# Turning attention probabilities with VectorE squares and a round trip through DRAM in place of TensorE transposes, in a two-layer decoder trunk

## The chip, the core and the metric

The kernel runs on one NeuronCore of a Trainium2 chip. The metric is the device time of one execution in microseconds (us). Engines are called by their names in the profile: PE is TensorE's matmuls, PEld its weight loads, DVE is VectorE, ACT is ScalarE, POOL is GpSimd, and SP is the engine that issues nearly all DMAs.

## What is computed

A decoder trunk of two layers over 256 positions of width 1024. Each layer adds to the residual, in this order, a mixer (self-attention with 16 heads of width 64), a cross-attention with 4 heads into a memory of 256 rows, and a gated MLP with a short convolution. The change concerns the mixer of the second layer, called layer 1 in the code, which is the forgetting attention of the reference:

```python
qpos = start + jnp.arange(Q_BLOCK)
s = (jnp.einsum('bhtd,bhsd->bhts', qb, k).astype(jnp.float32) * scale
     + cb[..., None] - c[:, :, None, :])
s = jnp.where(key_pos[None, :] <= qpos[:, None], s, NEG_INF)
p = jax.nn.softmax(s, axis=-1).astype(v.dtype)
return jnp.einsum('bhts,bhsd->bhtd', p, v)
```

`c` is a running sum of log forget gates. The softmax runs over keys. The last product sums over keys too, so on TensorE the probabilities are needed with keys on the partitions, while the softmax wants queries on the partitions. Between the two, each head's probabilities have to be turned. With the causal mask, a head has 128 queries that see 128 keys and 128 queries that see 256 keys: a tile of 128 partitions x 384 columns, which is three blocks of 128x128.

## The kernel before

Weights come from DRAM as blocks of 128x1024 float32 (512 KB), each loaded by one DMA of SP into a tile `raw` (7 buffers). `block` (line 127) loads one and splits it into a rounded part `whi` on ACT (line 135) and a remainder `wlo` on DVE (line 136), with 5 buffers each. A projection (`proj`, `proj_nat`) of 24 matmuls of 256 columns (line 347) uses them. `HALVES` (line 38) lists for some projections one matmul that is issued as two of 128 columns (line 345).

PE's instructions stand in the order of the program (`manual_schedule` near the end of `trunk`); the other engines' instructions are ordered by a scheduler, with the program's order as priority, and each engine then runs its own list strictly in order. SP's list holds the weight loads and all other DMAs.

`mixer` (line 650) works through the 16 heads as 8 pairs. A `Pipe` counts steps; a step ends with each projection (`pipe.tick()`), 2.72 us apart. In layer 1 the steps end, in this order, with: v0 (two steps), q1, k1, q2, k2 (step 6), v1 twice, q3 (9), k3 (10), q4 (11), k4, q5 (13), k5 (14), v2 twice (15, 16), q6, k6, q7 (19), k7 (20), v3 twice (21, 22), two projections of memory keys (23, 24), and the first output projections (25 and on). Here q3 is the query projection of pair 3, which holds two heads, and v1 the values of pairs 2 and 3.

`VISITS` (line 32) says at which step PE leaves the projections for attention work, and `visit` (line 671) does it. An entry is (step, out, prod, weigh), each a tuple of pairs:

- prod: `Soft.products` (line 459) multiplies queries by keys in plain float32, two matmuls for each head, into a PSUM bank `sc`. `Soft.scores` follows on other engines: DVE adds the decay and the mask and finds the maximum (line 468), ACT takes the exponential and its sum (line 472), DVE scales by the reciprocal of the sum (line 475). The result is the tile `s2` (`self.p`).
- weigh: `Soft.weigh` (line 477) has PE turn the tile by three 128x128 transposes into PSUM for each head (line 479), and ACT or DVE copy the result to a tile `pt` (line 481).
- out: `heads_out` (line 489) multiplies `pt` by the values (line 494), and ACT and DVE split the result into `gh` and `gl` (lines 499 and 501) for the output projection.

In layer 1, each couple of pairs goes through prod at steps 6, 11, 16 and 21, through weigh at 9, 14, 19 and 24, and through out at 11, 16, 21 and 26. `evac_row` (lines 396 and 398) brings q and k from PSUM on DVE; there are three PSUM banks `acc` for projections. `s2` and `pt` have four buffers of 384 columns each. The decay rows `bc` are read from DRAM by SP (line 614), and POOL works them up (line 615).

In the cross-attention (`cross`, line 868), `scores` makes the products of four heads with `Cross.products` (line 840), two matmuls of 256 columns for each head. They stand four matmuls into a projection of values, whose other 20 follow.

Late in layer 1's MLP, `move_blocks` (line 953) moves 32x32 squares between two on-chip tiles with 32 DMAs of 256 pieces of 128 bytes each (line 959); `turn_blocks` (line 950) turns 32x32 squares on DVE just before. `swap` (line 564) of layer 0 moves 32 partitions of 1024 bytes in each DMA (line 567).

Of the kernel before, what the change touches and what calls it, by code (L numbers as in the profile page):

```python
# [17 lines left out]
P = 128  # L18
# [62 lines left out]
def trunk(ctx: ExitStack, tc: tile.TileContext, a: dict, out: bass.AP):  # L81
# [45 lines left out]
    def block(src, cols=BLK, pieces=2):  # L127
        raw = wraw.tile([P, BLK], F32, tag="raw", name="raw")
        hi = wsp.tile([P, BLK], F32R, tag="whi", name="whi")
        lo = wsp.tile([P, BLK], F32R, tag="wlo", name="wlo")  # L130
        nc.sync.dma_start(raw[:, :cols], src)
# [12 lines left out]
        return Block(hi, lo)  # L144
# [270 lines left out]
    class Stick:  # L415
# [24 lines left out]
        def weigh(self, copy):  # L440
            z = self.z
            for sp in self.sp:
                nc.tensor.matmul(z, tri, sp, **ADD)  # L443
            for sp in self.sp:
                nc.tensor.matmul(z[:, P:T], negones, sp[:, T:384], **ADD)
            self.pt = tmp.tile([P, 384], F32, tag="pt", name="pt", bufs=4)
            nc.scalar.activation(self.pt, z, AF.Exp)

    class Soft:
# [11 lines left out]
        def scores(self):  # L461
# [3 lines left out]
            p = self.p = tmp.tile([P, 384], F32, tag="s2", name="s2", bufs=4)  # L465
# [11 lines left out]
        def weigh(self, copy):  # L477
            for c in (0, P, T):
                nc.tensor.transpose(self.s[:, c:c + P], self.p[:, c:c + P], ident)  # L479
            self.pt = tmp.tile([P, 384], F32, tag="pt", name="pt", bufs=4)  # L480
            copy(self.pt, self.s)


    def both_products(heads):
        steps = [hd.products() for hd in heads]
        while steps:
            steps = [i for i in steps if next(i, i) is not i]
# [162 lines left out]
    def mixer(layer, st, xs):  # L650
# [10 lines left out]
        heads = [None] * 8  # L661
# [9 lines left out]
        def visit(out, prod, weigh):  # L671
# [4 lines left out]
            for n in prod:  # L676
                q, k, _ = pairs[n]
                heads[n] = [Stick(i, q, k) if layer == 0 and n < 4 else
                            Soft(i, q, k, decays[2 * n + i] if decays else None) for i in range(2)]
            both_products([hd for n in prod for hd in heads[n]])  # L680
# [7 lines left out]
            for n in prod:  # L688
                for hd in heads[n]:
                    hd.scores()  # L690

# [9 lines left out]
        for g in range(4):  # L701
            def pair(i, hooks=({}, {})):
                wi = w[6 * g + 4 * i:6 * g + 4 * i + 2]
                pr = 2 * g + i
                q = early if layer == 0 and g == 1 and i == 0 else proj(block(wi[0]), 0, xs, accA(), hooks=hooks[0],
                                                                        halve=halves(f"q{pr}"))
                if hooks[0]:
                    return q, lambda: proj(block(wi[1]), 0, xs, accA(), hooks=hooks[1], halve=halves(f"k{pr}"))
# [8 lines left out]
                k = proj(b[3] if layer == 0 and g == 1 and i == 0 else block(wi[1]), 0, xs, accA(),  # L717
# [61 lines left out]
            def values():  # L779
                b = [block(w[6 * g + 2]), block(w[6 * g + 3])]  # L780
# [15 lines left out]
        ks = mem_keys(layer, ms, pipe)  # L796
# [3 lines left out]
        while j < 4:  # L800
            b = block(w_out[j])
# [12 lines left out]
        bo = [block(w_out[j])]  # L814
        for i in range(j, KD):
            if i < KD - 1:
                bo.append(block(w_out[i + 1]))
# [7 lines left out]
    def mem_keys(layer, ms, pipe):  # L825
        ks = []
        for i in range(2):
            ps = proj(block(a["xa_k"][layer, i]), 0, ms, accA(), halve=() if i else HALVES[layer].get("mk", ()))
# [4 lines left out]
    class Cross:  # L833
# [3 lines left out]
        def products(self):  # L837
            s = self.s = bank(psS, "sc")
            for t in range(2):
                nc.tensor.matmul(s[:, t * T:(t + 1) * T], self.q[:, t * P:(t + 1) * P], self.k, start=t == 0,  # L840
                                 stop=True, skip_group_check=True)
# [26 lines left out]
    def cross(layer, st, xs, ms, ks):  # L868
# [167 lines left out]
    def down_rows(gs, acc, spare):  # L1036
# [22 lines left out]
        def square(ps, s, scale=1.0):  # L1059
            n = ps.shape[1]  # L1060
            x = wide("sq") if n > 384 else tmp.tile([P, 384], F32, tag="s2", name="sq", bufs=4)
# [154 lines left out]
```

## Time and profile before

| | us |
|---|---|
| median of 3 runs | 648.34 (648.24 to 648.74) |
| profiled execution | 648.27 |
| span of that execution, first to last instruction | 646.5 |
| busy in the span: PE / DVE / ACT / POOL | 640.0 / 533.1 / 433.3 / 71.4 |

The page gives times in microseconds. Matmuls are pipelined: the length of one matmul in the trace is longer than the distance to the next, so a stream is read from its starts, or from the chain of waits, which merges equal instructions into pieces with a start, a length and a count. A DMA has two times: how long SP is busy with issuing it, and how long after that the data has landed. All times below are on the clock of the profiled execution, from its first instruction.

### The profile page before, as it was taken

What the parts mean: (1) busy time and instruction counts of PE and PEld (TensorE: products, weight loads), DVE (VectorE), ACT (ScalarE), POOL (GpSimd) and SP (SyncE); (2) the same over time, 40 slices, a digit from 0 to 9 for tenths busy, and PEclk for the clock granted to TensorE, in tenths of its full rate; (3) what the DMA queues carried; (4) which work ended last, traced back from release to release, by engine and by line L of the source; (5) the groups of instructions that cost most, each with busy time, mean ns of one, the idle gap of its engine ahead of it and who ended that gap; (6) DMA issues with size and microseconds to landing.
All of it is one profiled execution on the core that took longest, in us unless ns stands there. A gap on an engine that the chain in (4) does not pass through costs nothing.

```text
span 646.5 us, 14603 instructions
## 1 busy us (share of the span) xinstructions
PE 640.0 (99%) x5629; PEld 626.5 (97%) x5629; DVE 533.1 (82%) x1116; ACT 433.3 (67%) x871; POOL 71.4 (11%) x83
## 2 busy tenths in 40 slices
PE   9999999999999999999999999999999999999996
PEld 7999999999999999999999999999999999999996
DVE  7769995999999999766588987779999999996442
ACT  7689864688787676644464776557878666774332
POOL 0001000317000000011003220022450000000000
PEclk9999999999999999999999999999999999999999
DMA  8975751545556676666638754325365577595501
GB/s 338 388 273 196 268 190 46 195 153 204 185 169 219 210 216 181 182 194 199 212 126 301 254 179 139 131 86 180 122 236 193 165 225 201 163 357 197 193 2 66
DMA packets 47669, 125.07 MB, mean 193 GB/s; under 512 B 13520, under 2 KB 17392, under 8 KB 47600
## 3 DMA queue, kind: packets, MB, share of 16 engines
q1 hardware_dynamic: 47456, 123.88, 58.4%
q8 instruction: 44, 0.72, 0.4%
q10 hardware_dynamic: 144, 0.26, 0.1%
q14 instruction: 25, 0.20, 0.1%
HBM read 120.95 MB, written 1.07 MB: 189 GB/s over the span
## 4 chain that ended last, share of the span: by engine, by line
PE 98%; issue 1%; ACT 0%; DVE 0%; POOLq 0%; POOL 0%; DVEq 0%
PE acc L347 50%; PE sc L347 29%; PE acc L1053 3%; PE sc L1053 3%; PE po L1053 2%; PE po L494 2%; PE po L347 2%; PE sc L459 1%; PE sc L479 1%; PE sc L840 1%; PE sc L863 1%; PE acc L250 1%; PE sc L443 1%; PE po L899 0%; PE acc L345 0%
## 5 line engine op out<-in xcount | busy, mean ns | idle before, releaser
L136 DVE TENSOR_TENSOR wlo<-raw,whi 128x512 fp32r<-128x512 f32 (+2 forms) x288 | 267.6, 951 | 55.3 <-ACT whi L135 53.6
L135 ACT ACTIVATE whi<-raw 128x512 fp32r<-128x512 f32 (+2 forms) x288 | 225.4, 815 | 85.0 <-PE acc L347 34.1
L347 PE MATMUL sc<-xn,whi 128*128 128x256 f32 x656 | 112.9, 276 | 0.0
L347 PEld LDWEIGHTS sc<-xn,whi 128*128 128x128 f32 x656 | 98.6, 188 | 0.0
L347 PE MATMUL sc<-xn,wlo 128*128 128x256 f32 x328 | 90.5, 276 | 0.0
L347 PE MATMUL acc<-xh,whi 128*128 128x256 f32 x288 | 81.0, 281 | 0.0
L347 PE MATMUL acc<-xn,whi 128*128 128x256 f32 x464 | 80.3, 276 | 0.0
L347 PE MATMUL acc<-xl,whi 128*128 128x256 f32 x288 | 79.7, 277 | 0.0
L347 PE MATMUL acc<-xh,wlo 128*128 128x256 f32 x282 | 78.1, 277 | 0.0
L347 PEld LDWEIGHTS acc<-xn,whi 128*128 128x128 f32 x464 | 69.8, 188 | 0.0
L347 PE MATMUL acc<-gh,whi 128*128 128x256 f32 x240 | 66.9, 279 | 0.0
L347 PE MATMUL acc<-gl,whi 128*128 128x256 f32 x240 | 66.1, 277 | 0.0
L347 PE MATMUL acc<-gh,wlo 128*128 128x256 f32 x236 | 65.1, 276 | 0.0
L347 PE MATMUL acc<-xn,wlo 128*128 128x256 f32 x232 | 64.0, 276 | 0.0
L267 POOL TENSOR_TENSOR sq<-sq 128x256 f32<-128x256 f32 x35 | 30.1, 859 | 302.0 <-ACT sq L261 280.7
L347 PEld LDWEIGHTS sc<-xn,wlo 128*128 128x128 f32 x328 | 61.6, 188 | 0.0
L347 PEld LDWEIGHTS acc<-xh,whi 128*128 128x128 f32 x288 | 54.1, 188 | 0.4
L347 PEld LDWEIGHTS acc<-xl,whi 128*128 128x128 f32 x288 | 54.2, 188 | 0.0
L347 PEld LDWEIGHTS acc<-xh,wlo 128*128 128x128 f32 x282 | 53.0, 188 | 0.4 <-issue 0.4
L347 PEld LDWEIGHTS acc<-gh,whi 128*128 128x128 f32 x240 | 45.1, 188 | 1.1 <-ACT gh L185 0.8
L347 PEld LDWEIGHTS acc<-gl,whi 128*128 128x128 f32 x240 | 44.9, 188 | 0.0
L347 PEld LDWEIGHTS acc<-gh,wlo 128*128 128x128 f32 x236 | 44.3, 188 | 0.0
(310 smaller groups left out, 1536.7 us busy)
## 6 DMA issues: line engine op xcount, KB each, us to landing
raw<-up SPq DMA_DIRECT2D x88, 512.0 KB, 3.9
raw<-fox_in SPq DMA_DIRECT2D x24, 512.0 KB, 4.2
raw<-down_rows SPq DMA_DIRECT2D x22, 512.0 KB, 4.5
raw<-ab_in SPq DMA_DIRECT2D x20, 512.0 KB, 6.6
raw<-down SPq DMA_DIRECT2D x16, 448.0 KB, 3.5
raw<-ab_out SPq DMA_DIRECT2D x8, 512.0 KB, 4.8
raw<-down SPq DMA_DIRECT2D x8, 512.0 KB, 3.5
raw<-fox_out SPq DMA_DIRECT2D x8, 512.0 KB, 4.4
```

Of the source, the lines that this page charges most:

```text
L135: i = nc.scalar.activation(hi[:, s], raw[:, s], AF.Copy)
L136: j = nc.vector.tensor_sub(lo[:, s], raw[:, s], hi[:, s].bitcast(F32))
L250: nc.tensor.matmul(ps, w.broadcast_to([P, P]), w.broadcast_to([P, 512]), start=True, stop=True)
L267: nc.gpsimd.tensor_tensor(sq, sq, self.acc, op=ALU.add)
L347: nc.tensor.matmul(ps, st, mv, **kw)
L443: nc.tensor.matmul(z, tri, sp, **ADD)
L459: nc.tensor.matmul(s[:, c], q[:, qs], k[:, 0:n], start=i == 0, stop=True, skip_group_check=True)
L479: nc.tensor.transpose(self.s[:, c:c + P], self.p[:, c:c + P], ident)
L494: nc.tensor.matmul(po[i * DH:(i + 1) * DH, j * T + q:(j + 1) * T], v[m][:, vc + i * DH:vc + (i + 1) * DH], hd.pt[:, c], start=m == 0 and j ...
L840: nc.tensor.matmul(s[:, t * T:(t + 1) * T], self.q[:, t * P:(t + 1) * P], self.k, start=t == 0, stop=True, skip_group_check=True)
L863: nc.tensor.transpose(self.s[:, m * T + t * P:m * T + (t + 1) * P], self.p[:, t * T + m * P:t * T + (m + 1) * P], ident)
L1053: nc.tensor.matmul(ps[:, o:o + T], x[:, s], y[:, c + o:c + o + T], start=False, stop=k == KF - 1 and x is gl, skip_group_check=True)
```

## The change

Layer 1's probabilities of pairs 0 to 5 are no longer turned by PE. DVE turns each 32x32 square of a pair's tile in place (`nc.vector.transpose`), once for each pair, at the end of its scores. Four DMAs of SP for each pair then store the tile to DRAM (`store`, the entry's new field `away`), and four DMAs fetch it back (`fetch`, field `back`) into `pt`, so that the squares land in their turned places. A store DMA takes 32 partitions and writes 768 pieces of 128 bytes; a fetch DMA reads 192 pieces of 512 bytes. The last couple of pairs, 6 and 7, is still turned by PE at step 24.

The visits of layer 1 become: prod at 6, 11, 16 and 21 as before; out one round later, at 16, 21, 24 and 26; stores at 10, 15 and 20; fetches at 13, 19 and 22. Standalone visits of PE at 9, 14 and 19 are gone. Tiles `s2` and `pt` become two buffers of 768 columns, one for a pair.

In layer 1's mixer, weight loads are written six blocks ahead in the program (`weights`, `loads`), and each store and fetch is ordered behind the last load written so far. The pace of the loads is still set by the buffers of `raw`.

Matmuls issued in halves: in layer 1, the entry of `v2` goes and one for `k4` comes. In the cross-attention of both layers, the second row block of the last two heads' products is issued as two matmuls of 128 columns.

```diff
-          ((6, (), (0, 1), ()), (9, (), (), (0, 1)), (11, (0, 1), (2, 3), ()), (14, (), (), (2, 3)),
-           (16, (2, 3), (4, 5), ()), (19, (), (), (4, 5)), (21, (4, 5), (6, 7), ()), (24, (), (), (6, 7)),
-           (26, (6, 7), (), ())))
+          ((6, (), (0, 1), ()), (10, (), (), (), (0, 1)), (11, (), (2, 3), ()), (13, (), (), (), (), (0, 1)), (15, (), (), (), (2, 3)),
+           (16, (0, 1), (4, 5), ()), (19, (), (), (), (), (2, 3)), (20, (), (), (), (4, 5)),
+           (21, (2, 3), (6, 7), ()), (22, (), (), (), (), (4, 5)), (24, (4, 5), (), (6, 7)), (26, (6, 7), (), ())))
+TURNED = ((), (0, 1, 2, 3, 4, 5))
...
-          {"k0": (5,), "q1": (2,), "v1": (2,), "v2": (3,), "q6": (2,), "mk": (2,), "o2": (2,)})
+          {"k0": (5,), "q1": (2,), "v1": (2,), "k4": (2,), "q6": (2,), "mk": (2,), "o2": (2,)})
...
+    def of_pair(tag):
+        both = tmp.tile([P, 768], F32, tag=tag, name=tag, bufs=2)
+        return both, [both[:, i * 384:(i + 1) * 384] for i in range(2)]
+
+    def store(both, behind):
+        away = far.tile([32, 4 * 768], F32, tag="turn", name="turn", bufs=6)
+        to = away.rearrange("c (n i r) -> c n i r", i=4, r=32)
+        for i in range(4):
+            x = both[i * 32:i * 32 + 32].rearrange("c (n r) -> c n r", r=32)
+            order(nc.sync.dma_start(to[:, :, i], x), behind)
+        return away
+
+    def fetch(away, behind):
+        both, halves = of_pair("pt")
+        away = away.rearrange("c (s f q) -> c s f q", f=4, q=P)
+        for f in range(4):
+            i = nc.sync.dma_start(both[f * 32:f * 32 + 32].rearrange("c (s q) -> c s q", q=P), away[:, :, f])
+            order(i, behind)
+        return halves
...
+        def weights(src):
+            if layer == 0:
+                return block(src)
+            begun.append(src)
+            while len(loads) < min(len(begun) + 6, len(uses)):
+                loads.append(load(uses[len(loads)]))
+            return block(None, raw=loads[len(begun) - 1][0])
...
+            for n in away:
+                tiles[n] = store(tiles[n], loads[-1][1])
+            for n in back + weigh:
+                for hd, pt in zip(heads[n], fetch(tiles[n], loads[-1][1]) if n in back else of_pair("pt")[1]):
+                    hd.pt = pt
...
+                if n in TURNED[layer]:
+                    nc.vector.transpose(tiles[n], tiles[n])
...
-            both_products(hd[2:])
+            both_products(hd[2:], ((0, 0, T), (1, 0, P), (1, P, T)))
```

More of the change, by code (lines that the diff above doesn't have):

```diff
@@ L125, in fence, with load, block @@
         fences.append([skip, on_act, on_dve])
-    def block(src, cols=BLK, pieces=2):
+    def load(src, cols=BLK):
         raw = wraw.tile([P, BLK], F32, tag="raw", name="raw")
+        return raw, nc.sync.dma_start(raw[:, :cols], src)
+    def block(src, cols=BLK, pieces=2, raw=None):
+        if raw is None:
+            raw, _ = load(src, cols)
         hi = wsp.tile([P, BLK], F32R, tag="whi", name="whi")
         lo = wsp.tile([P, BLK], F32R, tag="wlo", name="wlo")
-        nc.sync.dma_start(raw[:, :cols], src)
         step = cols // pieces
@@ L660, in mixer @@
         pairs, turned = [None] * 8, [None] * 8
-        heads = [None] * 8
+        heads, tiles = [None] * 8, [None] * 8
+        first_soft = 0 if layer else 4
         def launch(pr, q, k, v):
@@ L669, in launch, with visit @@
                     pipe.at(d + (pr in (4, 6)), lambda x=x, r=r: (rope_sum if pr > 4 else rope)(x, r))
-        def visit(out, prod, weigh):
+        uses = [6 * g + i for g in range(4) for i in ((0, 1, 2, 3, 4, 5), (0, 1, 4, 5, 2, 3))[g > 1]]
+        uses = [w[i] for i in uses] + [a["xa_k"][layer, i] for i in range(2)] + [w_out[i] for i in range(KD)]
+        loads, begun = [], []
+        def weights(src):
[5 more added lines that the diff above has]
+            return block(None, raw=loads[len(begun) - 1][0])
+        def visit(out, prod, weigh, away=(), back=()):
             if out:
@@ L704, in pair @@
                 pr = 2 * g + i
-                q = early if layer == 0 and g == 1 and i == 0 else proj(block(wi[0]), 0, xs, accA(), hooks=hooks[0],
+                q = early if layer == 0 and g == 1 and i == 0 else proj(weights(wi[0]), 0, xs, accA(), hooks=hooks[0],
                                                                         halve=halves(f"q{pr}"))
                 if hooks[0]:
-                    return q, lambda: proj(block(wi[1]), 0, xs, accA(), hooks=hooks[1], halve=halves(f"k{pr}"))
+                    return q, lambda: proj(weights(wi[1]), 0, xs, accA(), hooks=hooks[1], halve=halves(f"k{pr}"))
                 if layer == 0 and pr > 4:
@@ L716, in pair @@
                 pipe.tick()
-                k = proj(b[3] if layer == 0 and g == 1 and i == 0 else block(wi[1]), 0, xs, accA(),
+                k = proj(b[3] if layer == 0 and g == 1 and i == 0 else weights(wi[1]), 0, xs, accA(),
                          halve=halves(f"k{pr}"))
@@ L779, in values @@
             def values():
-                b = [block(w[6 * g + 2]), block(w[6 * g + 3])]
+                b = [weights(w[6 * g + 2]), weights(w[6 * g + 3])]
                 for t in range(2):
@@ L795, in mixer @@
         assert len(ms) == KD
-        ks = mem_keys(layer, ms, pipe)
+        ks = mem_keys(layer, ms, pipe, weights)
         nst, nxt = Stats(one=True), Normed(h, G_XA + 8 * layer, "x", NX, 2)
@@ L800, in mixer @@
         while j < 4:
-            b = block(w_out[j])
+            b = weights(w_out[j])
             n = min(7, sum(o is not None for o in outs))
@@ L823, in mixer, with mem_keys @@
         return nst, nxt.res, ms, ks
-    def mem_keys(layer, ms, pipe):
+    def mem_keys(layer, ms, pipe, weights):
         ks = []
         for i in range(2):
-            ps = proj(block(a["xa_k"][layer, i]), 0, ms, accA(), halve=() if i else HALVES[layer].get("mk", ()))
+            ps = proj(weights(a["xa_k"][layer, i]), 0, ms, accA(), halve=() if i else HALVES[layer].get("mk", ()))
             ks.append(evac_row(ps, mem, "mk", False))
@@ L835, in __init__, with products @@
             self.q, self.k, self.st = q[HALF[i]], k[HALF[i]], st
-        def products(self):
+        def products(self, cuts=((0, 0, T), (1, 0, T))):
             s = self.s = bank(psS, "sc")
-            for t in range(2):
-                nc.tensor.matmul(s[:, t * T:(t + 1) * T], self.q[:, t * P:(t + 1) * P], self.k, start=t == 0,
-                                 stop=True, skip_group_check=True)
+            for t, c, e in cuts:
+                nc.tensor.matmul(s[:, t * T + c:t * T + e], self.q[:, t * P:(t + 1) * P], self.k[:, c:e],
+                                 start=t == c == 0, stop=True, skip_group_check=True)
                 yield
```

18 lines of the change are left out of this document (10 added, 8 removed).

## The prediction, written before the change was run

> **What bounds the kernel now.** I read the page first, then the chain of waits in order of time around the second mixer and the cross-attentions, then DVE, SP and the landing times of DMAs there. The page:
>
> ```profile
> span 646.5 us, 14603 instructions
> PE 640.0 (99%) x5629; PEld 626.5 (97%) x5629; DVE 533.1 (82%) x1116; ACT 433.3 (67%) x871; POOL 71.4 (11%) x83
> PE 98%; issue 1%; ACT 0%; DVE 0%; POOLq 0%; POOL 0%; DVEq 0%
> ```
>
> PE is never waiting for long: 98% of the chain that ended last is PE's own work. Time is saved only by giving PE less work or letting the same matmuls follow each other more tightly, and it is saved fully only while nobody else becomes late. The chain in the second mixer and in both cross-attentions (start, length, what, count):
>
> ```profile
> 128.39 2.56 PE po L347 x20
> 130.95 2.83 PE acc L347 x24
> ...
> 347.44 1.51 PE sc L459 x16
> 348.95 0.43 PE acc L347 x2
> 349.38 0.17 PE acc L345 x2
> 349.55 7.99 PE acc L347 x69
> 357.54 1.31 PE sc L479 x12
> 358.85 5.46 PE acc L347 x48
> 364.30 1.45 PE po L494 x16
> 365.76 1.51 PE sc L459 x16
> 367.26 8.38 PE acc L347 x72
> 375.64 1.31 PE sc L479 x12
> 376.95 0.36 PE acc L347 x3
> 377.31 0.17 PE acc L345 x2
> 377.48 5.04 PE acc L347 x44
> ...
> 393.98 1.31 PE sc L479 x12
> 395.29 5.47 PE acc L347 x48
> ...
> 437.12 5.44 PE sc L347 x48
> ...
> 445.28 2.56 PE po L347 x20
> 447.83 2.83 PE acc L347 x24
> ```
>
> Two readings. A visit that turns two pairs is 12 transposes in 1.31 us, 109 ns each. And the weight stream has two rhythms: 48 matmuls in 5.44 us are 113 ns each, while 24 in 2.83 us are 118 ns each. The slower one sets in after some switch between float32 and rounded work and stays until something shifts the stream; issuing one matmul in halves does that and costs next to nothing.
>
> **The change, part by part.**
>
> *Transposes removed.* Three visits (357.54, 375.64, 393.98) of 1.31 us: 3.93 us off PE's path. Nothing on PE replaces them.
>
> *Switches removed.* Each visit also disturbed the stream behind it. 48 matmuls cost 5.44 us when clean. After the first visit they took 5.46 (0.02 more); after the second 0.36 + 0.17 + 5.04 = 5.57 (0.13 more); after the third 5.47 (0.03 more). Together 0.18 us.
>
> *Out moved.* The product with the values (1.45 us) leaves step 11 and comes in at step 24, ahead of the transposes of the last couple. Its matmuls are the same; one float32 block is split off and another is joined on. I charge 0.1 us for a different switch, between 0 and 0.2.
>
> *Rhythm of the longer stretches.* Before, 69 matmuls at 349.55 took 7.99 us where 69 x 0.1133 = 7.82 are clean: a slow run of 0.17 us. Now five projections in a row follow each visit. If such a run begins in one of them it lasts until the next visit: at 0.11 us for 24 matmuls (2.83 less 2.72), up to 0.55 for each of three stretches. The entries at v1, k4 and q6 are issued in halves, which should start them clean. I charge 0.2, with bounds of -0.17 (the old run goes) and 1.65.
>
> *Cross scores in halves.* After the scores of a cross-attention, 20 + 24 matmuls run in the slow rhythm: 44 x 4.5 ns = 0.2 us in each layer. The second mixer's products end in 128-column matmuls and one stretch after them, the 72 at 367.26, is nearly clean (8.38 against 8.16, of which 0.11 is the entry). With the same ending I expect most of it back: 0.3 us for both layers, bounds 0 and 0.4. The four added instructions split streaming that is there anyway: about 0.
>
> *DVE's six turns.* A row for 256 columns exists:
>
> ```profile
> L951 DVE STREAM_TRANSPOSE mem<-h x8: 437/443/445, 493.3 to 528.2; 128x256 f32<-128x256 f32 x8
> 347.20:419.00 71.80, 71.80 (x651) 68.50 (x649) 59.63 (x195) 48.06 (x136) 13.74 (x16) 1.00 0.57 191
> ```
>
> 768 columns are three of these, 1.3 us at most; if part of the 0.44 is a fixed cost they are cheaper. Six are at most 8 us. The second row is the windows view for the second mixer: 71.80 us, of which DVE (its third figure) is busy 59.63. With 8 us more in a stage that is 4 us shorter, DVE would have 67.6 of 67.7 us: full, but not over. It hides because weight splits run several blocks ahead of PE, so lateness is absorbed; at zero cover each missing microsecond is PE's. ACT loses the copies of the three visits, which hides nothing on PE.
>
> *Stores and fetches on SP.* These DMAs' forms do not occur before. The nearest rows:
>
> ```profile
> 543.41 14.79 SPq L959 DMA_DIRECT2D h<-mem  x22
> ...
> L959 SPq DMA_DIRECT2D h<-mem x32: 591/608/1281, 528.8 to 557.6; - x32
> ...
> DMA to landing us min/median/max: 1.9/2.2/4.6
> ...
> L567 SPq DMA_DIRECT2D turned<-q x16: 507/582/1186, 50.1 to 80.7; - x16
> ...
> L131 SPq DMA_DIRECT2D raw<-fox_in x24: 328/328/516, 298.8 to 364.5; - x24
> ```
>
> A DMA of 256 pieces of 128 bytes (line 959) keeps SP for 0.61 us and the next follows after 0.67; one of 32 pieces (line 567) keeps it for 0.58; a weight load for 0.33. So eight times the pieces cost 0.03 us, and I take 0.7 us for a store of 768 pieces. Bounds: 0.33 (the load) and 2.0 (three pitches of 0.67, if pieces do set it). For a fetch of 192 pieces I take 0.65. Landing on chip took 2.2 us in the middle; through DRAM there are two rows, the store of the gate sums and the reads of the decays:
>
> ```profile
> L605 SPq DMA_DIRECT2D decay<-fc x1: 343/343/343, 339.3 to 339.3; - x1
> ...
> DMA to landing us min/median/max: 4.0/4.0/4.0
> ...
> L614 SPq DMA_DIRECT2D bc<-decay x16: 320/374/1373, 343.7 to 370.2; - x16
> ...
> DMA to landing us min/median/max: 3.9/5.2/5.9
> ```
>
> So a store lands 2.2 to 4.0 us after its issue, a fetch 2.2 to 5.2. The Trainium skill, "DMA: Bandwidth & Descriptors", section Specifications, says that transfers under 512 bytes miss line rate, being done as read-modify-write; that speaks against stores in 128-byte pieces. No run here has such writes to DRAM, so the trace neither agrees nor disagrees yet. By the rows above the sum keeps its terms; by the rule it goes towards the second rival's time, below.
>
> *Does the round trip fit?* The scores' ends and the evacuation of k3 on DVE:
>
> ```profile
> 356.14 0.55 DVE L475 TENSOR_SCALAR s<-s,sm 128x256 f32<-128x256 f32 x2
> ...
> 362.87 0.41 DVE L398 TENSOR_TENSOR k<-acc,rrow 128x256 f32<-128x256 f32 x1
> ...
> 391.55 0.55 DVE L475 TENSOR_SCALAR s<-s,sm 128x256 f32<-128x256 f32 x2
> ...
> 359.14 5.70 SPq L131 DMA_DIRECT2D raw<-fox_in  x4
> ```
>
> New times of PE's visits, with five clean projections (13.6 us) and 0.2 between: the first products end at 348.95 as before, the second at 348.95 + 13.8 + 1.5 = 364.3, the third (with out, 1.45) at 381.1, the fourth at 397.9.
>
> Round one: scores ended at 356.7; with two turns 359.3. Eight stores end at 362.6 (the first four begin earlier), landing 364.8 to 366.6. The scores of pairs 2 and 3 want the two `s2` tiles from 364.3 and some 1.2 us later: DVE waits 0 to 1 us, and evacuations and splits wait behind it, covered by three `acc` banks.
>
> Round three is the tightest. In the trace scores end at 392.1, 6.6 us after products that end at 365.76 + 1.51 + 8.38 + 1.31 + 5.57 + 1.45 + 1.51 = 385.5. New: 381.1 + 6.6 + 2.6 for turns = 390.3; the second pair's four stores end 393.1 and land by 397.1 at the latest. The fetch needs `pt` from the out at step 21, free at 396.4; eight fetches at 0.65 end at 401.6 to 402.3 and land 403.8 to 407.5. Out at step 24 wants them at 397.9 + three projections (8.16) + 0.1 = 406.2. Margin: 2.4 to -1.3 us. I take no wait, and keep 1.3 in the range. Round two has `pt` free at 379.5 and is wanted at 395, so it fits.
>
> Weight loads queue on SP behind these waits. The last four of the mixer's own loads are out by 364.84 (359.14 + 5.70), and the first of them, q7, is multiplied from 381.1 + 0.2 + 5.44 = 386.7 in the new order; with such a lead a stop of 10 us on SP reaches nobody.
>
> *Sum.* -3.93 - 0.18 + 0.1 + 0.2 - 0.3 = -4.1 us. The profiled execution is 648.27 (span 646.5 and 1.8 around it), 0.07 under the median of 648.34. From 648.3: 644.2 us.
>
> **The rivals.**
>
> *k3 is late at step 11.* Now out no longer stands between k3 and the products of pairs 2 and 3. They start at 362.8; in the trace k3 left PSUM on DVE at 362.87 + 0.41 = 363.3, behind splits, and two turns of up to 1.3 us now stand ahead of it. PE would wait 0.5 us, or 3.1 with the turns. For: the row. Against: q3 and k3 are done earlier too, and the list of DVE may be ordered otherwise. It gives 644.7 to 647.3, in the middle 646.
>
> *The stores are dear (slower).* If pieces set the price, at 2.0 us for each store, round three runs: first pair turned 389.0, eight stores to 405, landing 3.1, eight fetches 5.2, landing 3.7: 417.0 against 406.2. PE waits 10.8 us at step 24: 644.2 + 10.8 = 655, and 0.5 us more for each round that is late before it. It decides from the point where the wait eats the 4.1 us: 389.0 + 8s + 12.0 = 410.3, so s = 1.2 us. The skill's rule on 512 bytes leads here if it makes the store's transfer, not its issue, 2 us long. Against: the comparison of 32 with 256 pieces.
>
> *DVE is full.* At 1.3 us each turn DVE has no idle time left, yet 12.2 us were idle (71.80 less 59.63), much of it waiting for PE or ACT. Where a third of that stays, about 4 us, PE pays it: 648.2, no change. Against: turns below 1.3 us, and splits with blocks of lead.
>
> **How the numbers follow.** Forecast as summed, with the bounds of its terms: 0.60, from 643.5 (all terms at their good end: 3.93 + 0.18 + 0.4 + 0.17 = 4.68) to 645.7 (fetch late by 1.3 and more slow rhythm). k3 late: 0.17. DVE full: 0.12, of which a quarter ends below 647.0. Stores dear: 0.11. A difference of 0.2%, 1.3 us, is about what a measurement of this kernel can tell from no change. Faster: 0.60 + 0.17 + 0.03 = 0.80; same: 0.09; slower: 0.11. The range 643.5 to 647.4 holds the forecast, the first rival and the better quarter of the third: 0.80.
>
> **What would show it.** Right: 36 fewer transposes on PE; five projections as one piece of about 13.6 us; store issues near 0.7 us; DVE's turns at 0.9 to 1.3; PE's idle time before line 494 under 1 us; 44 matmuls after the cross scores in 5.2 us instead of 5.39 (2.56 + 2.83). Wrong: idle PE ahead of line 459 at step 11 (first rival), ahead of line 494 with a DMA as its releaser (second), or ahead of weight matmuls with DVE as releaser (third). A store issue over 1.2 us would overturn the forecast.

## The result and the profile after

| | us |
|---|---|
| before, median of 6 runs | 648.61 (648.24 to 648.95) |
| after, median of 6 runs | 653.61 (653.39 to 655.41) |
| ratio, 95% interval | 1.0084 (1.0073 to 1.0095) |
| span before / after | 646.5 / 651.7 |

The forecast was 644.2, range 643.5 to 647.4: the kernel is slower, by 5.0 us (0.8%, clear of the interval), and the forecast misses by 9.4. The page of the changed kernel, the lines that answer to those of before:

```profile
span 651.7 us, 14626 instructions
...
PE 639.2 (98%) x5601; PEld 624.5 (96%) x5601; DVE 537.8 (83%) x1122; ACT 428.9 (66%) x859; POOL 70.4 (11%) x83
...
PE 90%; DMA 3%; DVE 3%; issue 1%; ACT 1%; POOL 0%; SPq 0%; POOLq 0%; DVEq 0%; ACTq 0%
```

PE's part of the chain fell from 98% to 90%; DMAs and DVE took its place. Where, the chain of waits shows (start, length, what, count), from step 11 to the transposes of step 24:

```profile
364.33 1.15 PE sc L463 x12
366.08 13.34 PE acc L352 x117
379.42 1.45 PE po L516 x16
380.87 1.51 PE sc L463 x16
382.99 13.34 PE acc L352 x117
...
405.42 5.55 DMA raw<-fox_out
410.99 3.58 DMA pt<-turn
414.57 0.09 issue
414.66 1.97 PE po L516 x12
416.63 1.91 PE sc L483 x12
```

The middle is as forecast: five projections as one piece, 117 matmuls in 13.34 us, with out and the products between. At step 24 the chain leaves PE. It runs through a weight load (`raw<-fox_out`), which a fetch (`pt<-turn`) waited for, and through that fetch, which out (line 516) waited for. PE is done with step 23 at 409.3 and has the last pair's probabilities only at 414.6. The last two pieces are stretched as well: 12 transposes take 1.91 us here and 1.31 before, and the windows view gives a granted clock (third figure from the end) below 1. The first line is the kernel before, the others are the changed one:

```profile
347.20:423.00 75.80, 75.80 (x685) 72.48 (x684) 60.39 (x197) 48.72 (x138) 13.74 (x16) 1.00 0.55 184
...
347.20:423.00 75.80, 69.98 (x604) 65.47 (x604) 63.97 (x200) 43.12 (x123) 12.80 (x16) 0.98 0.90 244
...
412.00:425.00 13.00, 10.99 (x88) 9.35 (x89) 7.48 (x23) 7.17 (x20) 0.00 (x0) 0.87 0.95 342
```

In the mixer PE is busy for 69.98 of 75.80 us, where it had been busy all the time, and the DMA engines are busy for 0.90 of it, before for 0.55. The step 24 transposes end at 418.55, before the change at 413.54: the whole difference arises inside the mixer.

The price of each new instruction is what had been forecast. The views of the store's line and of the turn's line (ns, minimum, median, maximum):

```profile
L495 SPq DMA_DIRECT2D turn<-s x24: 550/656/3439, 356.9 to 404.0; - x24
...
DMA to landing us min/median/max: 2.5/3.1/8.0
...
L736 DVE STREAM_TRANSPOSE s<-s x6: 970/976/979, 355.9 to 400.6; 128x768 f32<-128x768 f32 x6
```

So the question is why prices that were right add up to a loss. The list of DVE in round three gives the first clue (start, length, what; idle time before it and what ended it):

```profile
382.51 2.06 DVE L195 SCALAR_TENSOR_TENSOR gl<-mem,small,gh 128x256 fp32r<-128x256 f32 x5
384.49 1.28 DVE L141 TENSOR_TENSOR wlo<-raw,whi 128x512 fp32r<-128x512 f32 x2
385.70 0.41 DVE L401 SCALAR_TENSOR_TENSOR q<-acc,rrow 128x256 f32<-128x256 f32 x1
386.08 1.29 DVE L141 TENSOR_TENSOR wlo<-raw,whi 128x512 fp32r<-128x512 f32 x2
388.20 0.42 DVE L403 TENSOR_TENSOR k<-acc,rrow 128x256 f32<-128x256 f32 x1 [0.83 <-PE acc L352]
390.92 0.42 DVE L401 SCALAR_TENSOR_TENSOR q<-acc,rrow 128x256 f32<-128x256 f32 x1 [2.29 <-PE acc L352]
391.26 0.41 DVE L472 CUSTOM_DVE_ANT_0 s<-sc,bc 128x256 f32<-128x256 f32 x1
```

The products of pairs 4 and 5 are ready at 382.4, and pair 2's last store, which holds the tile that pair 4 wants, landed at 383.0. Yet DVE looks at the scores (line 472) only at 391.26, and idles 0.83 and 2.29 us ahead of that, waiting for PE to finish projections whose evacuations stand earlier in its list. Pair 5 follows at 396.4. The tiles are free and DVE is idle: what is late is the place of the scores in the list.

### The profile page after: what moved, and what is told of

The parts are those of the page before. It is cut to its first block, busy times and chain, and to the rows that moved or that the text cites. A ratio compares the mean times of both kernels' runs of the same rounds, so it can differ in the third digit from the quotient of the medians.

```text
span 651.7 us, 14626 instructions
## 1 busy us (share of the span) xinstructions
PE 639.2 (98%) x5601; PEld 624.5 (96%) x5601; DVE 537.8 (83%) x1122; ACT 428.9 (66%) x859; POOL 70.4 (11%) x83
## 4 chain that ended last, share of the span: by engine, by line
PE 90%; DMA 3%; DVE 3%; issue 1%; ACT 1%; POOL 0%; SPq 0%; POOLq 0%; DVEq 0%; ACTq 0%
PE acc L352 44%; PE sc L352 28%; PE acc L1099 3%; PE sc L1099 3%; PE po L1099 2%; PE po L516 2%; PE po L352 2%; PE sc L463 1%; DVE wlo L141 1%; DMA bc<-decay 1%; ACT whi L140 1%; DMA raw<-fox_out 1%; PE sc L483 1%; PE sc L886 1%; PE sc L909 1%
## 5 line engine op out<-in xcount | busy, mean ns | idle before, releaser
L141 DVE TENSOR_TENSOR wlo<-raw,whi 128x512 fp32r<-128x512 f32 (+2 forms) x288 | 264.5, 941 | 50.5 <-ACT whi L140 49.4
```

## The experiments

All times are medians, and each ratio is to the kernel before, timed on the same chip.

### Without the trip

`a_no_trip` issues no stores and no fetches; out reads a tile filled with a constant. `a2_no_fetch` keeps the stores and leaves only the fetches out.

```diff
-            for n in away:
-                tiles[n] = store(tiles[n], loads[-1][1])
...
-                for hd, pt in zip(heads[n], fetch(tiles[n], loads[-1][1]) if n in back else of_pair("pt")[1]):
+                for hd, pt in zip(heads[n], blank() if n in back else of_pair("pt")[1]):
```

> The changed kernel without the round trip: no stores, no fetches; the product with the values of pairs 0 to 5 reads a tile that POOL fills with a constant, so this part of the computation is left out. DVE's turns, the visits of PE and all else stay. First theory (the two pair tiles of s2 hold the scores back: the next round's scores have to wait for the stores, DVE's list puts them behind other work, and the delay adds up to step 24): without stores the tiles are free at once, 644 to 646 us. Second theory (the trip itself, SP's issues and the landings, is too long for a round): also 644 to 646. Third theory (DVE is full, or PE's own path is longer than summed): 648 or more.

Measured: 645.89 (645.47 to 646.38), ratio 0.9957 (0.9942 to 0.9972). PE has no stall in the mixer. This is what the change is worth when nothing is late: 2.6 us, not the 4.1 of the forecast. Part of the gap is the slow rhythm, in the chain of this kernel, for the same 117 matmuls in its three long stretches; the other two lines are the products of step 11 and the transposes of step 24, which took 1.51 and 1.31 us before:

```profile
349.64 13.63 PE acc L352 x117
363.27 1.64 PE sc L463 x16
...
365.52 13.84 PE acc L352 x117
...
382.93 13.34 PE acc L352 x117
...
409.18 1.46 PE sc L483 x12
```

> As the run without the round trip, but with the stores kept: only the fetches are left out, and the product with the values reads the constant tile. First theory: the stores still hold the s2 tiles, so the scores of pairs 6 and 7 are still late and PE waits for them at step 24: 648 to 651 us. Second theory: what PE waited for were the fetches, SP has 24 issues less, so 645 to 646.

Measured: 658.86 (658.42 to 659.63), ratio 1.0158 (1.0143 to 1.0173). Less work, and 5 us slower than the whole change. The waits of PE name the scaling of pairs 6 and 7 at step 24:

```profile
PE sc L483 <- DVE s L479: 7.5, 2, 4.3
```

The program explains it: pair 7's tile was put into the memory of pair 6's, with the other tile free, so its scores wait until PE has transposed pair 6 (in the trace pair 7's first maximum, at 418.48, is released by those transposes). The scheduler chooses these places along with the order. So the run says nothing of the stores' price, but it shows that leaving a transfer out moves more than that transfer.

### More tiles

`b_three_tiles` adds a third tile for a pair over constants that this layer doesn't need, `d1_four_tiles` a fourth over a buffer of layer 0's scores. `d2_four_late` puts out of pairs 4 and 5 at step 25 as well, and `d6_four_late_q3` halves a matmul in q3 of that.

```diff
-                    tiles[n], ps = of_pair("s2")
+                    tiles[n], ps = pair_tile(layer, n)
...
-           (21, (2, 3), (6, 7), ()), (22, (), (), (), (), (4, 5)), (24, (4, 5), (), (6, 7)), (26, (6, 7), (), ())))
+           (21, (2, 3), (6, 7), ()), (22, (), (), (), (), (4, 5)), (24, (), (), (6, 7)), (25, (4, 5), (), ()), (26, (6, 7), (), ())))
```

> The changed kernel complete, with a third pair tile for s2, placed over constants that layer 1's mixer no longer uses; pairs 2 and 5 use it. First theory: a store has a round or nearly so to land before its tile is wanted, the scores come earlier on DVE, and most of the wait at step 24 goes: 645 to 648 us. Second theory: the trip is as long as before, 651 to 654.

> The changed kernel complete, with four pair tiles for s2: the third over constants no longer used, the fourth over the buffer of the first mixer's exponentials. Each tile is wanted again only two rounds after it was stored. First theory (too few tiles: the store's landing stands in the way of the next scores): scores follow their products at once, as in the run without the trip (645.9); what is left is the last fetch ahead of step 24, 1 to 3 us, so 646 to 649. Second theory (the trip itself is too long for a round): the three-tile run has taken what there is, 650 or more.

> As the run with four tiles, and the product with the values of pairs 4 and 5 one step later, at step 25, behind the first output projection. First theory: the last fetch has some 2 us more, the rest of the wait goes: 645.5 to 647.5. Second theory: PE waits for the fetch at step 25 as long as it did at 24, less 2 us.

> As the run with four tiles and the later product, with one matmul of the query projection of pair 3 issued in halves, where the slow rhythm of 118 ns sets in. If the rhythm is shifted back there, the 71 matmuls that follow lose 0.3 us: 0.3 us faster than the run without it. If not, the same.

Measured: 650.64 (ratio 1.0030, 1.0009 to 1.0051), 652.05 (1.0046, 1.0029 to 1.0063), 648.30 (0.9997, 0.9987 to 1.0007) and 647.72 (0.9990, 0.9978 to 1.0002), ten runs each, spread over 3 to 7 us. With four tiles DVE's list does have both pairs' scores together (383.5 to 386.2 in round three), and still PE waits 3.5 us at step 24 for the fetches. The reason stands in SP's list of `d1`:

```profile
385.17 8.54 SPq L514 DMA_DIRECT2D pt<-turn  x8
393.81 0.96 SPq L130 DMA_DIRECT2D raw<-fox_out  x1
394.87 6.80 SPq L507 DMA_DIRECT2D turn<-s  x8
```

DVE has turned pair 4 by 389.1 and pair 5 by 392.1, but SP is still issuing round two's fetches, and the stores stand behind them: they run from 394.87 to 401.67. So early scores alone were not enough: SP's list is a second place where the round is late. One step more for the fetches gave the loss back, but no gain: 648.30 misses the 645.5 to 647.5 expected. `d6` asked about rhythm: with a matmul of q3 in halves the first long stretch stays at 113 ns for each matmul to its end, where in `d2` it falls to 118, but in `d6` the next stretch runs at 118 instead, and the two medians differ by less than their spread.

### Order by force, and longer rows

`c_forced` puts all evacuations on DVE behind the last maximum of the scores. `d5_long_rows` forces no order and has each store write 32 rows of 3072 bytes in place of 768 pieces of 128; the squares then come back in the wrong places, so it computes another product.

```diff
-        to = away.rearrange("c (n i r) -> c n i r", i=4, r=32)
+        to = away.rearrange("c (i x) -> c i x", i=4)
         for i in range(4):
-            x = both[i * 32:i * 32 + 32].rearrange("c (n r) -> c n r", r=32)
-            order(nc.sync.dma_start(to[:, :, i], x), behind)
+            order(nc.sync.dma_start(to[:, i], both[i * 32:i * 32 + 32]), behind)
```

> The changed kernel complete, two tiles, but on DVE the evacuation of every later projection of queries or keys is ordered behind the last maximum of the scores that were issued before it. First theory, if it is the order on DVE that costs and not the landing itself: scores of round three start some us earlier, 646 to 650 us. If the landing of the stores is the limit, or by the second theory: 651 or more, with evacuations late in addition.

Measured: 655.12 (654.15 to 655.19), ratio 1.0099 (1.0083 to 1.0116). The scheduler now put turns and splits between the two pairs, and the evacuations behind them kept PE from its banks:

```profile
PE acc L352 <- DVE mx L476: 5.5, 2, 3.7
```

> The changed kernel with two tiles, but each store writes rows of 3072 bytes as they lie, 32 pieces in place of 768 of 128 bytes, so the probabilities come back in a wrong order and this part of the output is not the reference's. If pieces under 512 bytes make the stores slow (the rule of the Trainium skill, DMA: Bandwidth & Descriptors, Specifications), SP's issues and the landings get clearly shorter and the time falls by some us, towards 648. If pieces are not the price, issue stays near 0.6 us, landings near 3 us; then the time stays at 652 or more, unless the scheduler, which may count the pieces, makes another list.

Measured: 645.98 (645.71 to 646.29), ratio 0.9961 (0.9946 to 0.9976), as fast as without any trip, though 24 stores and 24 fetches move the same bytes. Stores are cheaper (issue 0.42 us, landing 1.8 to 6.1), but DVE's list in round three is another one too:

```profile
382.47 2.06 DVE L195 SCALAR_TENSOR_TENSOR gl<-mem,small,gh 128x256 fp32r<-128x256 f32 x5
384.45 0.42 DVE L472 CUSTOM_DVE_ANT_0 s<-sc,bc 128x256 f32<-128x256 f32 x1
```

The same row of line 195 as above, and the scores stand directly behind it, at 384.45 and not 391.26. Compared instruction by instruction, the two programs have the same order on PE, SP and GpSimd; only DVE's and ACT's differ. So two things changed at once: the transfer, and the scheduler's order.

### The order and the pieces apart

`e2_short_new_list` is the changed kernel with DVE's and ACT's instructions chained by hand in the order of `d5_long_rows`; `e3_long_old_list` is the reverse, long rows in the order of the changed kernel. In the traces DVE and ACT of `e2` run the same list as in `d5`, and those of `e3` the same as in the changed kernel.

```diff
+ON_DVE = (5458, ...
...
+    by = {i.name: i for i in nc.cur_bb.bb.instructions}
+    for numbers in (ON_DVE, ON_ACT):
+        for earlier, later in zip(numbers, numbers[1:]):
+            tc.add_manual_dep(by[f"I-{later}"], f"I-{earlier}", ...
```

> The changed kernel with its own transfers, pieces of 128 bytes on the stores, but with DVE's and ACT's instructions in the layer-1 mixer fixed by hand in the order in which the kernel with 3072-byte store rows has them; the lists of PE, SP and GpSimd are the same in both anyway. T-list (the scheduler's order is the loss: with the short pieces it puts the second pair's scores behind turns, evacuations and splits, though the chip has freed their tile long before): 645.8 to 646.8, no stall of PE over 0.6 us before step 24. T-landing (the pieces themselves are the loss: the stores' landing holds the tile, SP's queue and the fetches run late): 651 to 655, with DVE idle ahead of the second pair's maxima until a landing, and PE waiting for it. Both in part: the list gives rounds two and three back, and what is left is out's wait for the last fetches at step 24, 647.5 to 650.

> The kernel with 3072-byte store rows (its output is not the reference's: the blocks of the probabilities come back in the wrong places), with DVE's and ACT's instructions fixed in the order in which the changed kernel has them. T-list: 651 to 654, the pair of scores of round three again late and out at step 24 waiting for the fetches, as in the changed kernel. T-landing: 645.5 to 647, as with the list of its own. Both in part: 647.5 to 651.

| | order of the short pieces | order of the long rows |
|---|---|---|
| short pieces | 653.61 (the change) | 648.86 (`e2`; 646.99 to 653.16) |
| long rows | 655.14 (`e3`; 653.31 to 655.96) | 645.98 (`d5`) |

The ratios of the two new runs are 1.0015 (0.9998 to 1.0031) and 1.0099 (1.0086 to 1.0112). Along each row of the table, the order costs 4.8 us with short pieces and 9.2 with long rows. Down each column, the pieces cost nothing in the bad order (the long rows are even 1.5 slower) and 2.9 us in the good one. That 2.9 is not all the pieces' own: in `e2`'s profile PE also waits 0.6 us for ACT to clear a PSUM bank, which it does not in `d5`, and the runs of `e2` spread over 6 us. DVE in round three of `e3`, where the tile that pair 4 wants is free from 379.0 on:

```profile
388.86 0.42 DVE L425 TENSOR_TENSOR k<-acc,rrow 128x256 f32<-128x256 f32 x1 [0.73 <-PE acc L374]
391.58 0.42 DVE L423 SCALAR_TENSOR_TENSOR q<-acc,rrow 128x256 f32<-128x256 f32 x1 [2.29 <-PE acc L374]
391.92 0.41 DVE L494 CUSTOM_DVE_ANT_0 s<-sc,bc 128x256 f32<-128x256 f32 x1
```

It is the picture of the changed kernel to 0.7 us. The order is shown to be the main cause of the loss, since with either kind of store it moves the time by as much as the loss or nearly so. That the scheduler makes it because it counts the pieces of a store as a late landing is argued from the fact that nothing else differs.

### What the pieces still cost

`e4_list_out_late` gives `e2` the out at step 25. `e5_four_turned` sends only pairs 0 to 3 through DRAM; the diff is `e5`'s, and `e4` has the entries of `d2` for steps 24 and 25.

```diff
-           (16, (0, 1), (4, 5), ()), (19, (), (), (), (), (2, 3)), (20, (), (), (), (4, 5)),
-           (21, (2, 3), (6, 7), ()), (22, (), (), (), (), (4, 5)), (24, (4, 5), (), (6, 7)), (26, (6, 7), (), ())))
-TURNED = ((), (0, 1, 2, 3, 4, 5))
+           (16, (0, 1), (4, 5), ()), (19, (), (), (), (), (2, 3)), (20, (), (), (4, 5)),
+           (21, (2, 3), (6, 7), ()), (24, (4, 5), (), (6, 7)), (26, (6, 7), (), ())))
+TURNED = ((), (0, 1, 2, 3))
```

> The changed kernel, DVE's and ACT's lists again fixed as the kernel with long store rows has them, and out of pairs 4 and 5 one step later (25 in place of 24), so that the fetches of round three have some 2.8 us more. If, with that list, the only thing left of the loss is out's wait for the last fetches at step 24 (1.7 us of stalls in the profile of the run before, and more where the clock falls behind it): 645.8 to 647.0 and a spread of under 2 us. If stores or fetches also hold weight loads or tiles at other places: 647.5 to 650, with the spread of some 6 us that the two-tile kernel with the fixed list had.

> Only pairs 0 to 3 go through DRAM; pairs 4 and 5 are transposed by TensorE again at step 20, out at 24; lists fixed in the order that long store rows give. 12 transposes of 109 ns come back, 1.31 us on the 645.9 of the kernel without the trip: 647.2, range 646.6 to 647.8, with a spread of under 2 us if the trip of round three was the last thing that costs. If the trips of rounds one and two cost by themselves (tiles, SP's queue, weight loads behind them): 648.5 to 650.

Measured: 652.64 (1.0062, 1.0048 to 1.0076) and 655.11 (1.0101, 1.0088 to 1.0115), and neither answers its question. In both, the scheduler again put the second pair of a round into the first pair's tile, as in `a2_no_fetch`: the order was forced, the places were not. DVE in `e4`, pair 7's first maximum:

```profile
408.96 0.42 DVE L484 CUSTOM_DVE_ANT_0 s<-sc,bc 128x256 f32<-128x256 f32 x1 [3.95 <-PE sc L495]
```

`e6_own_slots_out_late` and `e7_own_slots_four_turned` repeat the two with a name for each tile.

```diff
-                    tiles[n], ps = of_pair("s2")
+                    tiles[n], ps = of_pair(("s2", "s3")[n % 2], 1)
```

> The kernel with the fixed lists and out of pairs 4 and 5 at step 25 once more, but now the two s2 pair tiles have names of their own (even and odd pairs), so that the scheduler can't put pair 7 into pair 6's tile, as it did in the run before, where pair 7's maxima waited 3.95 us for pair 6's transposes. If out's wait for the last fetches is what is left of the loss: 645.8 to 647.0, no stall of PE over 0.9 us in steps 11 to 25, spread under 2 us. If the short pieces also cost by landing late (tiles, weight loads): 647.5 to 649.5.

> Pairs 0 to 3 alone go through DRAM, pairs 4 and 5 are transposed by TensorE; lists fixed in the order that long store rows give, the two pair tiles with names of their own, so that pair 5 no longer sits in pair 4's tile (its maxima waited 4.55 us there, and PE 3.4 us). If the trip of round three was the only one that costs: 645.9 + 1.31 = 647.2, range 646.6 to 647.8. If the trips of rounds one and two cost as well: 648.5 to 650.

Measured: 647.73 (0.9993, 0.9982 to 1.0004) and 649.03 (1.0012, 1.0003 to 1.0021). The places were worth 4.9 and 6.1 us. By its own expectation `e7`'s 649.03 would mean that the trips of rounds one and two cost as well (647.2 if not), but 1.2 us of waits in its profile come from places and lists, so little of the difference is left for the trips. Both kernels still have two stalls: 0.45 us for k3 ahead of the second pair's products, and 0.73 us where PE waits for ACT to clear the PSUM bank that PE has just filled, again a place that the scheduler chose (read from the starts of the matmuls; the profile's list of waits gives 0.2 and 0.6). `e10_early_k_banks` takes these two out of `e6`: k3 and k5 leave PSUM two splits earlier, and the banks are taken in turn.

```diff
+            accs.append(0)
+            tag = f"acc{len(accs) % 3}"
+            return pl.tile([P, 512], F32, tag=tag, name=tag, bufs=1)[:, :width]
```

> The kernel with fixed lists, own names for the two pair tiles and out of pairs 4 and 5 at step 25, with its two remaining stalls of PE taken away: the evacuations of k3 and k5 stand two splits earlier in DVE's list (PE waited 0.45 us for k3 ahead of the second pair's products), and the three PSUM banks of the projections are taken strictly in turn (PE waited 0.73 us for ACT to clear the bank that it had just filled). If lists and places are the whole of the loss: 647.73 less 1.2 = 646.5, range 645.9 to 647.0, which is less than before's 648.6 by 0.3 per cent. If the short pieces hold weight loads or tiles here as well: no gain, 647.3 to 648.5.

Measured: 648.51 (1.0000, 0.9988 to 1.0013), runs from 645.76 to 651.20. The two stalls are gone, and no time was won. In the one profiled execution (647.69) PE waits 1.5 us at and behind steps 24 and 25, for ACT and DVE; where the slower runs lost their time is not known.

### Which pieces, and which queue

`e11_short_fetch` writes pieces of 512 bytes and reads pieces of 128, with the scheduler's own lists; `e12_short_fetch_late` adds out at step 25 and the tiles' names.

```diff
-        to = away.rearrange("c (n i r) -> c n i r", i=4, r=32)
+        to = away.rearrange("c (s i q) -> c s i q", i=4, q=P)
...
-        away = away.rearrange("c (s f q) -> c s f q", f=4, q=P)
+        away = away.rearrange("c (n f r) -> c n f r", f=4, r=32)
```

> The same transposition with the short pieces on the other side: the stores write pieces of 512 bytes and the fetches read pieces of 128 bytes, with nothing fixed by hand, the lists being the scheduler's own. Its DVE list then has the second pair's scores of round two right behind the first's, as with 3072-byte rows, and in round three behind two splits and an evacuation. If it is the short pieces of the stores, through the list and their landing, that cost: 646 to 648, less than the changed kernel by 6 or more, with what is left at out's wait for the fetches at step 24. If 128-byte pieces cost wherever they stand: 650 to 655, the fetches landing 2 us or more later and out at step 24 waiting for them.

> The same with out of pairs 4 and 5 at step 25 and the two pair tiles under names of their own. If the fetches of round three are all that is left in the run before: 645.9 to 647.0, faster than before by 0.25 per cent or more, with a spread under 2 us. If stores of 512 bytes still hold the tiles in round three: 647.5 to 649.5.

Measured: 653.63 (1.0067, 1.0053 to 1.0082) and 649.79 (1.0015, 1.0006 to 1.0024). `e12` is slower than both of its expectations (645.9 to 647.0, 647.5 to 649.5). In `e11` the scores of pair 4 come at 387.4, between the good and the bad order, and the last fetch lands at 413.1, with PE waiting 4.6 us at step 24. From the last store's issue to the last landing `e11` takes 13.7 us, and the other kernels of the table below 9.9 to 11.8: short pieces cost on the reading side too.

Side by side, round three of the kernels that have out at step 24 (us; PE gets there between 407.7 and 409.7):

| | pair 4's scores | last store issued | last fetch landed | median |
|---|---|---|---|---|
| after | 391.3 | 404.0 | 414.6 | 653.61 |
| `e3`, long rows, old order | 391.9 | 403.9 | 414.6 | 655.14 |
| `e11`, short fetches | 387.4 | 399.4 | 413.1 | 653.63 |
| `d1`, four tiles | 383.5 | 401.0 | 412.8 | 652.05 |
| `e2`, short, new order | 384.8 | 398.3 | 409.8 | 648.86 |
| `d5`, long rows, new order | 384.5 | 396.8 | 406.6 | 645.98 |

The time goes with the landing of the last fetch. And its chain has the same end in four of these kernels; in `e2`:

```profile
399.76 7.41 DMA raw<-fox_out
407.18 2.66 DMA pt<-turn
409.84 0.09 issue
409.93 1.09 PE po L527 x12
```

SP's list has two weight loads between the last stores and the fetches. In the program the DMAs take eight semaphores in turn, so that the last fetch is issued only when the load eight places before it has landed, and that takes 5.5 to 7.4 us. The chain makes this look dearer than it is: most of the load's flight passes while SP issues the other seven fetches anyway, and SP stands only 0.4 us for it in the changed kernel and 1.1 in `e2`. `e13_fetch_first` has names and banks of `e10`, lists made in the same way, out at step 24, and the two loads behind the fetches.

```diff
+            if back == (4, 5):
+                for _, load_of in loads[-2:]:
+                    order(load_of, fetched[-1])
```

> Short pieces and out at step 24 as in the changed kernel; lists fixed as long store rows give them, k3 and k5 evacuated two splits earlier, own names for the pair tiles and PSUM banks in turn, and in SP's list the eight fetches of round three ahead of the two weight loads that stood between them and the stores. In four profiles the chain into step 24 ends the same way: the last fetch waits 5.5 to 7.4 us for a weight load issued eight DMAs before it, then lands 2.7 to 3.7 us later. If that wait is what short pieces still cost: the last fetch lands by 408.5 us in place of 409.9 to 414.6, PE waits under 0.7 us at step 24, and the time is 646.0 to 647.2, below before by 0.2 to 0.4 per cent. If it is the pieces' own landing: the last fetch lands after 409.5, and the time is 647.5 to 649.

Measured: 647.35 (645.64 to 649.79), ratio 0.9984 (0.9974 to 0.9993), the first version with the whole trip that is faster than before, by 0.16%, just above the 646.0 to 647.2 expected. In its profiled execution, which took 645.64, PE waits for nothing in the mixer. SP's list and the chain:

```profile
392.25 7.00 SPq L513 DMA_DIRECT2D turn<-s  x8
399.43 5.55 SPq L522 DMA_DIRECT2D pt<-turn  x8
405.09 3.17 SPq L148 DMA_DIRECT2D raw<-fox_out  x6
```

```profile
407.60 1.45 PE po L537 x16
409.05 1.46 PE sc L501 x12
410.51 4.38 PE acc L370 x36
```

The last fetch is issued at 404.38, needs no load, and lands at 406.95, 0.6 us ahead of its use. From the last store's issue to that landing it takes 8.3 us, in `e2` 11.5: of the 3.2 us, 2.1 are SP's time for the two loads ahead of the first fetch and 1.0 the slower issue of the eight fetches, the wait for the load above all. No run has `e13`'s lists and places with the loads in their old place, so what the loads alone cost in the median is not shown. Other runs took up to 4 us more; that landings vary by more than this margin from run to run is the likely reason, but only one execution of each kernel has a trace, so this stays open.

## Why the prediction was wrong

The step that failed is in "Does the round trip fit?": *"In the trace scores end at 392.1, 6.6 us after products ... New: 381.1 + 6.6 + 2.6 for turns = 390.3; the second pair's four stores end 393.1"*. It carried the scores' length over from a kernel in which DVE's list held both pairs in one burst, pair 4's first maximum to pair 5's last in 2.6 us. Before, then the changed kernel with the second pair's turn and SP's stores:

```profile
386.24 0.42 DVE L468 CUSTOM_DVE_ANT_0 s<-sc,bc 128x256 f32<-128x256 f32 x1
...
388.52 0.29 DVE L468 CUSTOM_DVE_ANT_0 s<-sc,bc 128x128 f32<-128x128 f32 x1
...
400.63 0.97 DVE L736 STREAM_TRANSPOSE s<-s 128x768 f32<-128x768 f32 x1
...
396.50 8.14 SPq L495 DMA_DIRECT2D turn<-s  x8
```

In the changed kernel the products end at 382.4 and the second pair is turned at 401.6, 19.2 us later and not 9.2. The stores end at 404.6 instead of 393.1, and a margin that was put at 2.4 to -1.3 us became a lateness of 5 us or more. The prediction took the order of DVE's list as given, although the front of this document says that a scheduler makes it, and the change gave the scheduler new transfers to order around. The same step has a second gap, which `d1` lays open: there the list has its burst, the second pair is turned 9.4 us after the products, much as forecast, and still the stores end at 401.7, 8.6 us after the forecast's 393.1, because SP's own list, with round two's fetches ahead of the stores, was not followed.

Point by point:

- *Transposes, turns, issue prices* were right: 0.98 us for a turn (0.9 to 1.3 expected), 0.66 for a store's issue (0.7), 0.60 for a fetch's (0.65).
- *Landings* were bounded at 4.0 and 5.2 us. In rounds one and two stores took up to 8.0 us and fetches up to 8.6, when weight loads were in flight; in round three 2.5 to 3.4 and 3.6 to 5.2. The bounds failed where there was slack, and held where there was none.
- *Weight loads* were followed only one way: whether stores and fetches make them late. The runs show the other way: loads that make fetches late, by SP's time for their issue and, by 0.4 to 1.1 us, through the semaphore that a load and the last fetch share.
- *Rhythm*: 0.2 us charged; 0.50 in one stretch of `a_no_trip` and 0.29 in another (13.84 and 13.63 against 13.34), inside the bounds. The prediction's reading that a matmul in halves at the entry starts a stretch clean does not hold: the stretch of 13.84 us follows such an entry (k4).
- *Cross scores in halves*: 0.3 us expected, nothing measured. The chain after:

```profile
128.39 2.55 PE po L352 x20
130.94 2.83 PE acc L352 x24
```

  Before, these were 2.56 and 2.83. The 44 matmuls keep the slow rhythm.
- *k3 late at step 11*, the first rival, came true beside the rest: PE stands 0.4 us by the profile (0.7 from start to start) between the first and the second pair's products, the low end of the 0.5 to 3.1 forecast.
- *Stores are dear*, the second rival, had the right place (out at step 24, behind the fetches) and the right sign, by the wrong mechanism, so that its 655 comes near the measured 653.6 is chance: its condition, 1.2 us for each store, was not met at the median of 0.66 (single ones were held 2 to 3.4 us), and with long rows, which keep SP 0.37 us, the same lateness came from the order alone. The rule of the Trainium skill that stood beside it ("DMA: Bandwidth & Descriptors", Specifications: under 512 bytes no line rate) agrees in its sign, not in a size that decides: in round three, stores in 128-byte pieces land after 2.5 to 3.4 us, in rows of 3072 bytes (`e3`) after 1.8 to 2.3, and `e3` is no faster.
- *DVE is full*, the third rival, is refuted: it idles 2.29 us right ahead of the late scores.

The sum had an error of its own, beside the lateness: of the forecast's 4.1 us, `a_no_trip` gives 2.6 (2.8 from span to span, 646.5 to 643.7). The chains of the two kernels show the missing 1.3 us. Weight matmuls in the mixer, up to step 24, take 0.65 us more than before, where switches, moved out and rhythm were summed to 0.12. The products of step 11 and the transposes of step 24 take 0.13 and 0.15 more. The cross scores give nothing of their 0.3, and the PE pieces behind them (line 863 before, 912 in `a_no_trip`) take 1.98 us in each layer for 1.86. Why these pieces are longer is not shown. A slip beside it: the range's lower end follows from its terms as 648.3 - 4.68 = 643.6, not 643.5.

## What to carry to other kernels

When a scheduler orders an engine's list, a new transfer changes that order and the places of the tiles; the length of a stage must then be read from the new list, not carried over from the old trace. The list of the engine that issues the DMAs is such a list too. Before a DMA's landing is blamed, see whether its waiter stands late in its own engine's list, or the DMA itself waits for an older one. A run that takes work out can be slower, since order and places move with it: compare the lists before the times.

## What the runs showed of the hardware

- 24 stores of 96 KB cost SP 0.66 us each with 768 pieces and 0.37 to 0.42 with 32 rows; while the DMA engines were 0.9 busy (366 to 385) one store with 768 pieces held SP for 3.44 us, with 32 rows at most 1.07.
- After PE had stood for 3.3 us (the changed kernel) and 3.5 us (`e3`), the granted clock in the windows was below 1 (0.87 and 0.74, for 412 to 425), and 12 transposes took 1.91 and 2.75 us where they take 1.46 in `e13`, in which PE did not stand (clock 1.00 for 412 to 425). These stalls thus cost more than their own length.
